# Attention on one core: sums issued singly between other VectorE work, Q fetched a tile earlier

## The chip, the cores and the metric

The kernel runs on one core of a Trainium2 chip. The metric is the device time of one execution in microseconds. TensorE does the matrix products, ScalarE (ACT) the exponentials and copies out of PSUM, VectorE (DVE) the additions, GpSimd (POOL) issues the loads, and SyncE (SP) issues the transposing DMAs and the stores. The engines run side by side, each through its own instructions in order, and wait for one another by semaphores.

## The reference

For each of 8 batches there are q, k and v of 2048 x 512 (float32):

```
scores = q @ k.T / sqrt(512)
out = softmax(scores, axis=-1) @ v
```

The kernel works in float16 with float32 sums. It leaves out the maximum in the softmax and divides by the row's sum at the end; that sum comes from a column of ones beside v.

## The kernel before, in words

**The products.** Each large product is cut into 2 x 2 blocks and done with seven block products instead of eight (Strassen-Winograd). That needs sums of blocks of the operands, made on VectorE: four instructions of 128 x 512 float16 for a chunk of K (`k_sums`, lines 138 to 145), for a query tile (`q_sums`, 147 to 154), for a chunk of V (`v_sums`, 170 to 178), and for the exponentials (`p_sums`, 274 to 284).

**Tiles and stages.** A query tile is 512 rows; a batch has four, so there are 32. Stage g (1 to 31) multiplies the exponentials of tile g by V (class `Pair`) and, interleaved with that, makes the scores of tile g+1 (class `Group`). "Kind" means g modulo 4 below: it decides which prefetches a stage carries. A full stage has 28 slots (0 to 27). In each slot one block product of the scores is issued (four matmuls of 256 columns, line 237), in each odd slot also one block product of Pair (eight matmuls, line 319), and last the prefetches that a table gives for (kind, slot). Before stage 1, a prologue loads the first batch and does tiles 0 and 1 with plain matmuls.

**One turn of the scores.** A group of 256 keys takes seven slots, in the order `QORDER` (line 368), and two of its products (7 and 4) are done in the next group's turn. At slot 1 of a turn product 7 of the group before is issued, and VectorE adds it into a buffer (line 260, which ends the use of a PSUM bank that product 4 at slot 4 writes on). At slot 2 ScalarE takes the exponential of that buffer (`exp_right`, line 272, recorded as L188 pt<-cz). At slot 4 come three of the four `p_sums` (lines 280 to 282), which wait for that exponential; at slot 5 the second addition (line 263) and the fourth (line 284).

**Pair.** A tile's output is done as two halves, a and b, in the order `ORDER` (line 366): a1 b1 a5 a3 a2 a6 a7 b5 a4 b3 b2 b6 b7 b4, at slots 1, 3, 5, ... 27. After products 5 and 3 VectorE takes a reciprocal (lines 342, 348) and ScalarE scales (line 327); after 2, 6 and 7 VectorE adds scaled halves into the output tile ("final", line 330). Product 3 has to wait for the scaling after 5, product 7 for the scaling after 6, and product 4 for the final after 7, since they write on the same PSUM banks. There are four output tiles in rotation; a tile is free again when its store (line 337) has landed.

**Prefetch.** Lines 372 to 429. Loads cast to float16 on the way from memory, into three staging buffers for Q and K (line 62) or straight into V's two buffers (line 65). A transposing DMA (line 111) then turns Q or K into its operand, from SP's queue, where the stores stand too. SP and POOL run ahead of the slots: what holds them is the order of their queues and their waits. VectorE does the sums where the table's slot puts them in its queue, four in a row. Q's tile for stage g+1's scores, number g+2, is loaded at slot 0 of stage g, transposed at slot 9 and summed at slot 21. Q's operands have three buffers (line 64).

Of the kernel before, what the change touches and what calls it, by code (L numbers as in the profile page):

```python
# [1 line left out]

# [9 lines left out]
def kernel(  # L12
# [21 lines left out]
    nc = tc.nc  # L34
    P = 128
    B, T, D = q.shape
# [10 lines left out]
    NQT = T // QTW  # L47
# [3 lines left out]
    H = D // 2  # L51
# [45 lines left out]
    def load(what, b, c):  # L97
        t = stage.tile([P, CH, D], F16, tag="stage")
        nc.gpsimd.dma_start(out=t[:], in_=srcs[what][b, :, c * CH:(c + 1) * CH, :])
        staged[what, b, c] = t  # L100
# [7 lines left out]
    def dma_transpose(what, b, c):  # L108
        src = staged.pop((what, b, c))
        t = operands(what)  # L110
        nc.sync.dma_start_transpose(
            out=t[0][:].rearrange("p n c r -> p (n c) r"),
            in_=src[:].rearrange("p n d -> p (n d)"),
        )
        (kT if what == "k" else qT)[b, c] = t
# [14 lines left out]
    def k_blocks(t):  # L130
        w = t[0][:].rearrange("p (j s) c r -> p j s c r", s=2)
        return w[:, :, 0, 0:2], w[:, :, 0, 2:4], w[:, :, 1, 0:2], w[:, :, 1, 2:4]

    def q_blocks(t):
        w = t[0]
        return w[:, 0:2, 0:2], w[:, 2:4, 0:2], w[:, 0:2, 2:4], w[:, 2:4, 2:4]

    def k_sums(b, c):
        t = kT[b, c]
        a11, a12, a21, a22 = k_blocks(t)  # L140
        _, s1, s2, s4 = t
        nc.vector.tensor_add(s1[:], a21, a22)
        nc.vector.tensor_sub(a21, a11, a21)
        nc.vector.tensor_sub(s2[:], s1[:], a11)
        nc.vector.tensor_sub(s4[:], a12, s2[:])

    def q_sums(b, c):
        t = qT[b, c]
        b11, b12, b21, b22 = q_blocks(t)
        _, t1, t2, t4 = t  # L150
        nc.vector.tensor_sub(t1[:], b12, b11)
        nc.vector.tensor_sub(b12, b22, b12)  # L152
        nc.vector.tensor_sub(t2[:], b22, t1[:])
        nc.vector.tensor_sub(t4[:], b21, t2[:])  # L154

    def new_v(b):
        vh = vpool.tile([P, NJ, 2, VP], F16, tag="vh")
        t1 = vpool.tile([P, NJ, TP], F16, tag="t1")
        t2 = vpool.tile([P, NJ, H], F16, tag="t2")
        t4 = vpool.tile([P, NJ, H], F16, tag="t4")  # L160
        nc.gpsimd.memset(vh[:, :, 1, D:D + 1], 1.0)
        nc.gpsimd.memset(t1[:, :, H:H + 1], 1.0)
        vs[b] = (vh, t1, t2, t4)

    def load_v(b, c):
        dst = vs[b][0][:].rearrange("p j s d -> p (j s) d")
        ns = slice(c * CH, (c + 1) * CH)
        nc.gpsimd.dma_start(out=dst[:, ns, 0:D], in_=srcs["v"][b, :, ns, :])

    def v_sums(b, c):  # L170
        vh, t1, t2, t4 = vs[b]
        js = slice(c * CH // 2, (c + 1) * CH // 2)
        b11, b12 = vh[:, js, 0, 0:H], vh[:, js, 0, H:D]
        b21, b22 = vh[:, js, 1, 0:H], vh[:, js, 1, H:D]
        nc.vector.tensor_sub(t1[:, js, 0:H], b12, b11)
        nc.vector.tensor_sub(b12, b22, b12)
        nc.vector.tensor_sub(t2[:, js], b22, t1[:, js, 0:H])
        nc.vector.tensor_sub(t4[:, js], b21, t2[:, js])

    def new_p(g):  # L180
        pt = ppool.tile([P, NJ, 2, QTW], F16, tag="pt")
# [8 lines left out]
    def plain_tile(g, kb):  # L190

        b, qt = divmod(g, NQT)
        if kb == 0:
            new_p(g)
        st = bank("qz" if kb % 3 == 2 else "qx")
        c, n = divmod(kb, CH)
        for dc in range(ND):
            nc.tensor.matmul(  # L198
                st[:], kT[b, c][0][:, n, dc, :], qT[b, qt][0][:, :, dc, :],
                start=(dc == 0), stop=(dc == ND - 1),  # L200
            )
        exp(pts[g][0][:, kb // 2, kb % 2, :], st[:])
# [71 lines left out]
    def p_sums(g, n, part=None):  # L274
        pt, s1, s2, s4 = pts[g]
        js = slice(n * G, (n + 1) * G)
        a11, a21 = pt[:, js, 0, 0:QH], pt[:, js, 0, QH:QTW]
        a12, a22 = pt[:, js, 1, 0:QH], pt[:, js, 1, QH:QTW]
        if part in (None, 0):
            nc.vector.tensor_add(s1[:, js], a21, a22)  # L280
            nc.vector.tensor_sub(s2[:, js], s1[:, js], a11)
            nc.vector.tensor_sub(a21, a11, a21)  # L282
        if part in (None, 1):
            nc.vector.tensor_sub(s4[:, js], a12, s2[:, js])  # L284
# [83 lines left out]
    QORDER = ((0, 1), (1, 7), (0, 5), (0, 6), (1, 4), (0, 3), (0, 2))  # L368
    NS = len(QORDER) * NG


    def plan():
        at = {}

        def add(qt, slot, *what):
            at.setdefault((qt, slot), []).append(what)

        for qt in range(NQT):
            add(qt, 0, "load", "q", 3)
            add(qt, 9, "trans", "q", 3)  # L380
            add(qt, 21, "qsum", "q", 3)
        add(0, 1, "newv")
        for c, (lq, ls, sq, ss) in enumerate(((0, 1, 0, 14), (0, 5, 0, 25), (1, 1, 1, 14), (1, 5, 1, 25))):
            add(lq, ls, "load", "v", c)
            add(sq, ss, "vsum", "v", c)
        add(1, 15, "load", "k", 0)
        add(1, 25, "trans", "k", 0)
        add(2, 6, "ksum", "k", 0)
        add(2, 3, "load", "k", 1)
        add(2, 13, "trans", "k", 1)  # L390
        add(2, 26, "ksum", "k", 1)
        add(2, 11, "load", "k", 2)
        add(2, 20, "trans", "k", 2)
        add(3, 4, "ksum", "k", 2)
        add(2, 18, "load", "k", 3)
        add(2, 27, "trans", "k", 3)
        add(3, 11, "ksum", "k", 3)
        return at

    PLAN = plan()  # L400

    def prefetch(g, slot):
        b, qt = divmod(g, NQT)
        todo = PLAN.get((qt, slot), [])
        if g == 1:
            todo = [x for x in PLAN.get((0, slot), ()) if x[0] == "newv" or x[1] == "v"] + todo
        for what in todo:
            if what[0] != "newv" and what[1] == "q":
                n = g + 2
                if n >= B * NQT or n < NQT:  # L410
                    continue
                bb, c = divmod(n, NQT)
            else:
                bb = b + 1
                if bb >= B:
                    continue
                c = what[2] if len(what) > 2 else 0
            if what[0] == "newv":
                new_v(bb)
            elif what[0] == "load":  # L420
                load_v(bb, c) if what[1] == "v" else load(what[1], bb, c)
            elif what[0] == "trans":
                dma_transpose(what[1], bb, c)
            elif what[0] == "ksum":
                k_sums(bb, c)
            elif what[0] == "qsum":
                q_sums(bb, c)
            elif what[0] == "vsum":
                v_sums(bb, c)


    NP = B * NQT
# [31 lines left out]
    def pv(g, n):  # L464
        pairs[ORDER[n][0] == "b"].product(int(ORDER[n][1]))

    for kb in range(NKB):
        plain_tile(1, kb)
        if kb == 3:
            dma_transpose("q", 0, 2)  # L470
        if kb == 4:
            dma_transpose("q", 0, 3)
        if 6 <= kb < 14 and kb % 2 == 0:
            v_sums(0, (kb - 6) // 2)
        if kb % (2 * G) == 0 and kb:
            p_sums(1, kb // (2 * G) - 1)
        if kb >= 14:
            pv(0, kb - 14)
    p_sums(1, NG - 1)
    for n in range(2, len(ORDER)):  # L480
        pv(0, n)
        if n < 6:
            k_sums(0, n - 2)
        if n == 6:
            q_sums(0, 2)
        if n == 7:
            q_sums(0, 3)

    prev = None
    for g in range(1, NP):  # L490
        pairs = (Pair(g, 0), Pair(g, 1))
        for slot in range(NS):
            if g + 1 < NP:
                n, at = divmod(slot, len(QORDER))
                if at == 0:
                    cur = Group(g + 1, n)
                old, what = QORDER[at]
# [6 lines left out]
            if g + 1 < NP or slot < 7:  # L504
                at = slot % len(QORDER)
# [42 lines left out]
```

## Time and profile before

| What | Value |
|---|---|
| time, three runs | 950.77 us (949.81 to 951.2) |
| the profiled execution | 956.65 us, of it 954.6 us between its first and last instruction |
| granted TensorE clock, mean | 0.975 |
| TensorE, VectorE, ScalarE, GpSimd busy | 88%, 62%, 60%, 8% of the span |
| DMA queues | 115.50 MB moved, mean 121 GB/s |

The busy share is a mean over a prologue of some 65 us, 30 stages of 25.8 to 31.4 us and a short end. Stage g was delimited by the start of the first product of its slot 0 on TensorE's timeline; stages 1 to 29 carry sums of the prefetch, stage 30 carries none. In the timeline, rows of one line that follow one another are merged, and the bracket tells how long the engine sat idle before the row and what ended that.

### The profile page before, as it was taken

The page shows a single profiled execution, that of the slowest core. Times are in us where ns is not written, and L with a number is a line of the kernel's source. Part 1 is how long each engine was busy: PE and PEld are TensorE (multiplying, and loading weights), DVE is VectorE, ACT ScalarE, POOL GpSimd, SP SyncE. Part 2 cuts the span into 40 slices and gives each one's busy share as a digit, 9 for nine tenths or more (in the row PEclk, how much of TensorE's full clock was granted, in tenths as well). Part 3 has the DMA queues.
Part 4 walks back from the last instruction along what each step waited for, and adds up shares of the span by engine and source line. Part 5 has one row for each costly group of instructions (what it writes and reads, how often), then busy time and mean ns, then how long its engine had stood idle before and what let it go on. Part 6 is the DMA issues. An engine that isn't in the chain of part 4 may idle for free.

```text
span 954.6 us, 18101 instructions
## 1 busy us (share of the span) xinstructions
PE 843.9 (88%) x7169; PEld 709.0 (74%) x7169; DVE 593.1 (62%) x1460; ACT 569.2 (60%) x1009; POOL 72.8 (8%) x116
## 2 busy tenths in 40 slices
PE   6978998899898998988989889898889899899997
PEld 4567777677776777777878778687777787777885
DVE  3767656566665676567666576656666566666553
ACT  2525656566565665666656566565656656566673
POOL 3100001000010000100001000010001000000000
PEclk9999989999998999999999999999999999999999
DMA  9992957849687484974959659395693946931111
GB/s 145 202 162 74 139 109 122 155 91 142 123 133 137 99 151 101 144 144 97 153 83 157 135 108 155 73 174 120 119 155 77 181 98 106 184 90 43 52 41 67
DMA packets 189989, 115.50 MB, mean 121 GB/s; under 512 B 124368, under 2 KB 173520, under 8 KB 189904
## 3 DMA queue, kind: packets, MB, share of 16 engines
q0 software_dynamic: 50688, 50.34, 35.6%
q1 hardware_dynamic: 139216, 64.01, 31.2%
q8 instruction: 56, 0.92, 0.4%
q14 instruction: 29, 0.24, 0.1%
HBM read 100.70 MB, written 33.55 MB: 141 GB/s over the span
## 4 chain that ended last, share of the span: by engine, by line
PE 40%; DVE 25%; ACT 15%; DMA 14%; issue 5%; POOL 0%; ACTq 0%; DVEq 0%; POOLq 0%
PE t L319 20%; PE t L237 16%; DMA raw<-t 14%; ACT pt L188 7%; ACT o L327 5%; DVE o L330 4%; PE t L198 3%; DVE cz L260 3%; DVE cz L263 3%; ACT cz L254 2%; DVE s L280 2%; DVE pt L282 1%; DVE s L284 1%; DVE raw L152 1%; DVE qs L154 1%
## 5 line engine op out<-in xcount | busy, mean ns | idle before, releaser
L319 PEld LDWEIGHTS <-pt 128*128 128x128 f16 x2048 | 204.8, 100 | 69.8 <-issue 41.8
L237 PEld LDWEIGHTS <-raw 128*128 128x128 f16 x1920 | 189.8, 99 | 69.2 <-issue 45.3
L319 PE MATMUL t<-vh,pt 128*128 128x256 f16 x1536 | 207.1, 280 | 26.3 <-ACT o L327 26.3
L327 ACT ACTIVATE o<-t,r 128x256 f32<-128x256 f32 x256 | 121.5, 475 | 180.9 <-DVE r L342 107.9
L188 ACT ACTIVATE pt<-t 128x512 f16<-128x512 f32 x272 | 163.7, 602 | 83.9 <-PE t L237 57.4
L237 PE MATMUL t<-raw 128*128 128x256 f16 x1440 | 204.1, 276 | 7.7 <-ACT pt L188 7.7
L319 PEld LDWEIGHTS <-s 128*128 128x128 f16 x1536 | 150.5, 98 | 53.5 <-issue 33.4
L330 DVE SCALAR_TENSOR_TENSOR o<-t,r,o 128x256 f32<-128x256 f32 x192 | 92.5, 482 | 114.0 <-ACT o L327 81.2
L237 PEld LDWEIGHTS <-ks 128*128 128x128 f16 x1440 | 143.8, 100 | 23.6 <-issue 1.8
L188 ACT ACTIVATE pt<-cz 128x1024 f16<-128x1024 f32 x120 | 127.4, 1061 | 47.4 <-DVE cz L260 47.4
L237 PE MATMUL t<-qs,ks 128*128 128x256 f16 x960 | 137.2, 277 | 1.0 <-DVE cz L263 1.0
L280 DVE TENSOR_TENSOR s<-pt 128x512 f16<-128x512 f16 x128 | 54.1, 422 | 129.7 <-ACT pt L188 129.7
L319 PE MATMUL t<-t,s 128*128 128x257 f16 (+1 forms) x1024 | 133.1, 273 | 0.8 <-DVE o L330 0.8
L237 PE MATMUL t<-qs,raw 128*128 128x256 f16 x480 | 72.3, 273 | 29.1 <-DVE cz L260 29.1
L260 DVE TENSOR_TENSOR cz<-t,cz 128x512 f32<-128x512 f32 x120 | 82.4, 687 | 24.3 <-PE t L237 24.1
L254 ACT COPY cz<-t 128x512 f32<-128x512 f32 x120 | 70.2, 585 | 43.3 <-PE t L237 39.2
L319 PE MATMUL t<-vh,s 128*128 128x257 f16 x512 | 68.4, 277 | 27.8 <-ACT o L327 27.8
L263 DVE TENSOR_TENSOR cz<-t,cz 128x512 f32<-128x512 f32 x120 | 81.9, 682 | 5.6 <-PE t L237 5.6
L250 ACT COPY t<-t 128x512 f32<-128x512 f32 x120 | 68.4, 570 | 23.9 <-PE t L237 21.5
L237 PE MATMUL t<-raw,ks 128*128 128x256 f16 x480 | 75.4, 281 | 0.5 <-ACT cz L254 0.5
L319 PE MATMUL t<-t,pt 128*128 128x256 f16 x512 | 68.2, 277 | 5.0 <-DVE o L330 2.1
L257 ACT COPY cz<-t 128x512 f32<-128x512 f32 x120 | 69.6, 580 | 1.9 <-PE t L237 1.8
(34 smaller groups left out, 482.7 us busy)
## 6 DMA issues: line engine op xcount, KB each, us to landing
out_dram<-o SPq DMA_DIRECT2D x128, 256.0 KB, 2.5
t<-in_q_dram POOLq DMA_DIRECT2D x32, 512.0 KB, 8.2
t<-in_k_dram POOLq DMA_DIRECT2D x32, 512.0 KB, 7.5
vh<-in_v_dram POOLq DMA_DIRECT2D x32, 512.0 KB, 14.9
raw<-t SPq DMA_TRANSPOSE x58, 7.0
ident<-attn_identity SPq DMA_DIRECT2D x1, 32.0 KB, 1.6
```

What stands on the lines that cost most here:

```text
L188: nc.scalar.activation(out=out_, in_=in_, func=EXP, scale=inv_sqrt_d)
L198: nc.tensor.matmul(st[:], kT[b, c][0][:, n, dc, :], qT[b, qt][0][:, :, dc, :], start=(dc == 0), stop=(dc == ND - 1),)
L237: nc.tensor.matmul(dst[:, j * QH:(j + 1) * QH], lhs[:, j, c, :], rhs[:, :, c, :], start=(n in (1, 5) and j == 0 and c == 0), stop=(c == 1) ...
L250: nc.scalar.copy(out=self.y[:], in_=self.x[:])
L254: nc.scalar.copy(out=self.cz[:, :, 1, :], in_=self.two(self.z))
L257: nc.scalar.copy(out=self.cz[:, :, 0, :], in_=self.two(self.x))
L260: nc.vector.tensor_add(self.cz[:, :, 1, :], self.two(self.x), self.cz[:, :, 1, :])
L263: nc.vector.tensor_add(self.cz[:, :, 0, :], self.two(self.z), self.cz[:, :, 0, :])
L280: nc.vector.tensor_add(s1[:, js], a21, a22)
L319: nc.tensor.matmul(dst[:, 0:width], lhs(j), rhs(j), start=(first and j == 0), stop=(j == NJ - 1), skip_group_check=True,)
L327: nc.scalar.activation(out=out_, in_=src, func=COPY, scale=r[:])
L330: nc.vector.scalar_tensor_tensor(out=out_, in0=src, scalar=r[:], in1=out_, op0=MULT, op1=ADD)
```

## The change

There are three edits.

1. `k_sums`, `q_sums` and `v_sums` no longer issue their four instructions, but return them as a list. The prologue runs each list at once. In the stages the list is appended to a queue, `background`, and one instruction is taken from it at the end of slots 0, 2, 3 and 6 of each turn of seven.
2. The table has Q's load at slot 0 and its transpose at slot 10 for tile g+3, and its sums, appended at slot 12 (15 in stages of kind 3), for tile g+2, which was transposed one stage earlier.
3. The other entries of the table move by a few slots: the loads of V, the sums of V (14 and 25 become 16 and 24), the loads, transposes and sums of K. The preparation of V's next buffer (`new_v`, with two memsets on POOL) comes at slot 0, ahead of Q's load, instead of at slot 1, behind it.

The number of instructions and their sizes stay as they are.

```
     def k_sums(b, c):
...
-        nc.vector.tensor_add(s1[:], a21, a22)
-        nc.vector.tensor_sub(a21, a11, a21)
-        nc.vector.tensor_sub(s2[:], s1[:], a11)
-        nc.vector.tensor_sub(s4[:], a12, s2[:])
+        return [
+            lambda: add(s1[:], a21, a22),
+            lambda: sub(a21, a11, a21),
+            lambda: sub(s2[:], s1[:], a11),
+            lambda: sub(s4[:], a12, s2[:]),
+        ]
...
+    PLAN = {}
+    for qt_, slot_, *what_ in (
+        (0, 0, "newv"),
+        (0, 2, "load", "v", 0), (0, 16, "sum", "v", 0),
+        (0, 8, "load", "v", 1), (0, 24, "sum", "v", 1),
+        (1, 2, "load", "v", 2), (1, 16, "sum", "v", 2),
+        (1, 8, "load", "v", 3), (1, 24, "sum", "v", 3),
+        (1, 16, "load", "k", 0), (1, 26, "trans", "k", 0), (2, 8, "sum", "k", 0),
+        (2, 2, "load", "k", 1), (2, 14, "trans", "k", 1), (2, 25, "sum", "k", 1),
+        (2, 8, "load", "k", 2), (2, 20, "trans", "k", 2), (3, 4, "sum", "k", 2),
+        (2, 14, "load", "k", 3), (2, 27, "trans", "k", 3), (3, 11, "sum", "k", 3),
+    ):
+        PLAN.setdefault((qt_, slot_), []).append(what_)
+    for qt_ in range(NQT):
+        PLAN.setdefault((qt_, 0), []).append(("load", "q", 3))
+        PLAN.setdefault((qt_, 10), []).append(("trans", "q", 3))
+        PLAN.setdefault((qt_, 15 if qt_ == 3 else 12), []).append(("sum", "q", 2))
+    background = deque()
...
+                background.extend({"k": k_sums, "q": q_sums, "v": v_sums}[what[1]](bb, c))
+        if background and slot % len(QORDER) in (0, 2, 3, 6):
+            background.popleft()()
```

## Rows read from the trace of the kernel before

**Rows 1.** Page, part 1: busy time, share of the span, instructions of each engine.

```profile
PE 843.9 (88%) x7169; PEld 709.0 (74%) x7169; DVE 593.1 (62%) x1460; ACT 569.2 (60%) x1009; POOL 72.8 (8%) x116
```

**Rows 2.** Waits of TensorE: us in total, times, longest us.

```profile
PE t L319 <- ACT o L327: 54.1, 66, 2.1
PE t L237 <- DVE cz L260: 29.1, 29, 2.6
```

**Rows 3.** Windows, sums over stages: six of kind 0, 1, 2; seven of kind 3.

```profile
sum 184.57, PE 161.19 PEld 136.00 DVE 108.63 ACT 108.02 POOL 22.71; mean PE 26.86 PEld 22.67 DVE 18.11 ACT 18.00 POOL 3.78
...
sum 167.57, PE 152.75 PEld 131.45 DVE 106.58 ACT 108.01 POOL 4.44; mean PE 25.46 PEld 21.91 DVE 17.76 ACT 18.00 POOL 0.74
...
sum 163.25, PE 150.74 PEld 131.32 DVE 112.52 ACT 108.51 POOL 13.76; mean PE 25.12 PEld 21.89 DVE 18.75 ACT 18.09 POOL 2.29
...
sum 216.29, PE 187.68 PEld 158.19 DVE 139.82 ACT 126.50 POOL 14.26; mean PE 26.81 PEld 22.60 DVE 19.97 ACT 18.07 POOL 2.04
```

**Rows 4.** Windows: stage 2; stages 28 and 29 summed; stage 30 (start:end, length, busy, PEclk).

```profile
91.90:122.00 30.10, 26.79 (x226) 22.75 (x224) 20.99 (x52) 18.08 (x32) 2.96 (x4) 0.94 0.90 154
...
sum 54.41, PE 50.24 PEld 43.81 DVE 31.54 ACT 36.17 POOL 0.00; mean PE 25.12 PEld 21.90 DVE 15.77 ACT 18.09 POOL 0.00
...
908.09:933.90 25.81, 24.96 (x226) 21.91 (x224) 14.26 (x35) 17.98 (x32) 0.00 (x0) 1.00 0.11 43
```

**Rows 5.** Timeline, TensorE, ends of stages 29 and 30 (start, length, work, idle before).

```profile
903.73 0.60 PE L237 MATMUL t<-qs,raw 128*128 128x256 f16 x4 [0.63 <-DVE cz L260]
905.18 1.03 PE L319 MATMUL t<-vh,pt 128*128 128x256 f16 x8 [0.85 <-ACT o L327]
...
930.99 1.03 PE L319 MATMUL t<-vh,pt 128*128 128x256 f16 x8 [0.25 <-ACT o L327]
...
933.03 1.03 PE L319 MATMUL t<-t,pt 128*128 128x256 f16 x8
```

**Rows 6.** Timeline, VectorE, stage 29: three of Q's sums and the addition behind them.

```profile
901.86 0.42 DVE L152 TENSOR_TENSOR raw<-raw 128x512 f16<-128x512 f16 x1
902.20 0.42 DVE L153 TENSOR_TENSOR qs<-raw,qs 128x512 f16<-128x512 f16 x1
902.65 0.42 DVE L154 TENSOR_TENSOR qs<-raw,qs 128x512 f16<-128x512 f16 x1
902.99 0.68 DVE L260 TENSOR_TENSOR cz<-t,cz 128x512 f32<-128x512 f32 x1
```

**Rows 7.** Timeline, VectorE, stage 30, where no prefetch sums run.

```profile
922.03 0.69 DVE L260 TENSOR_TENSOR cz<-t,cz 128x512 f32<-128x512 f32 x1 [0.30 <-PE t L237]
...
925.05 0.42 DVE L280 TENSOR_TENSOR s<-pt 128x512 f16<-128x512 f16 x1 [1.97 <-ACT pt L188]
...
928.22 0.48 DVE L330 SCALAR_TENSOR_TENSOR o<-t,r,o 128x256 f32<-128x256 f32 x1 [0.93 <-ACT o L327]
928.62 0.68 DVE L260 TENSOR_TENSOR cz<-t,cz 128x512 f32<-128x512 f32 x1
930.97 0.48 DVE L330 SCALAR_TENSOR_TENSOR o<-t,r,o 128x256 f32<-128x256 f32 x1 [1.68 <-ACT o L327]
...
932.50 0.48 DVE L330 SCALAR_TENSOR_TENSOR o<-t,r,o 128x256 f32<-128x256 f32 x1
```

**Rows 8.** Timeline, ScalarE, stage 30: the exponential behind the last addition.

```profile
929.51 1.06 ACT L188 ACTIVATE pt<-cz 128x1024 f16<-128x1024 f32 x1
```

**Rows 9.** Timeline, TensorE, stage 7 (kind 3), product a3 at slot 7.

```profile
247.34 1.67 PE L319 MATMUL t<-vh,s 128*128 128x257 f16 x8 [2.05 <-ACT o L327]
```

**Rows 10.** Windows: the stretch behind that wait (the 0.50 is the granted clock).

```profile
247.59:251.00 3.41, 3.41 (x19) 2.40 (x17) 0.86 (x2) 1.48 (x4) 0.00 (x0) 0.50 1.34 167
```

**Rows 11.** Groups by line: the first of Q's sums.

```profile
L151 DVE TENSOR_TENSOR qs<-raw 128x512 f16<-128x512 f16 x30 | 12.5, 416 | 9.2 <-DMA raw<-t 9.2
```

**Rows 12.** Chain of waits, stage 8 (kind 0): Q's transposing DMA.

```profile
271.27 21.41 DMA raw<-t
```

**Rows 13.** DMA issues from 288 to 290 us: a store, KB, us to landing.

```profile
out_dram<-o SPq DMA_DIRECT2D x1, 256.0 KB, 6.5
```

More of the change, by code (lines that the diff above doesn't have):

```diff
@@ L1 @@
+from collections import deque
 from contextlib import ExitStack
@@ L136, in q_blocks @@
         return w[:, 0:2, 0:2], w[:, 2:4, 0:2], w[:, 0:2, 2:4], w[:, 2:4, 2:4]
+    add, sub = nc.vector.tensor_add, nc.vector.tensor_sub
     def k_sums(b, c):
@@ L150, in q_sums @@
         _, t1, t2, t4 = t
[L151 to L154, printed above, removed]
+        return [
+            lambda: sub(t1[:], b12, b11),
+            lambda: sub(b12, b22, b12),
+            lambda: sub(t2[:], b22, t1[:]),
+            lambda: sub(t4[:], b21, t2[:]),
+        ]
     def new_v(b):
@@ L174, in v_sums @@
         b21, b22 = vh[:, js, 1, 0:H], vh[:, js, 1, H:D]
[L175 to L178, printed above, removed]
+        return [
+            lambda: sub(t1[:, js, 0:H], b12, b11),
+            lambda: sub(b12, b22, b12),
+            lambda: sub(t2[:, js], b22, t1[:, js, 0:H]),
+            lambda: sub(t4[:, js], b21, t2[:, js]),
+        ]
     def new_p(g):
@@ L369 @@
     NS = len(QORDER) * NG
[L372 to L400, printed above, removed]
+    PLAN = {}
+    for qt_, slot_, *what_ in (
+        (0, 0, "newv"),
[8 rows of a table added]
+    ):
[5 more added lines that the diff above has]
+    background = deque()
     def prefetch(g, slot):
@@ L407, in prefetch @@
         for what in todo:
+            bb, c = b + 1, what[-1]
             if what[0] != "newv" and what[1] == "q":
-                n = g + 2
-                if n >= B * NQT or n < NQT:
+                if not NQT <= g + what[2] < B * NQT:
                     continue
[L412 to L417, printed above, removed]
+                bb, c = divmod(g + what[2], NQT)
+            elif bb >= B:
+                continue
             if what[0] == "newv":
@@ L423, in prefetch @@
                 dma_transpose(what[1], bb, c)
[L424 to L429, printed above, removed]
+            else:
+                background.extend({"k": k_sums, "q": q_sums, "v": v_sums}[what[1]](bb, c))
+        if background and slot % len(QORDER) in (0, 2, 3, 6):
+            background.popleft()()
     NP = B * NQT
@@ L473 @@
         if 6 <= kb < 14 and kb % 2 == 0:
-            v_sums(0, (kb - 6) // 2)
+            for f in v_sums(0, (kb - 6) // 2):
+                f()
         if kb % (2 * G) == 0 and kb:
@@ L482 @@
         if n < 6:
-            k_sums(0, n - 2)
+            for f in k_sums(0, n - 2):
+                f()
         if n == 6:
-            q_sums(0, 2)
+            for f in q_sums(0, 2):
+                f()
         if n == 7:
-            q_sums(0, 3)
+            for f in q_sums(0, 3):
+                f()
     prev = None
```

## The prediction, made before the change was run

> **What bounds the kernel now.** I read the page's busy shares first: TensorE is busy 88% of the span, VectorE and ScalarE about 60% [rows 1]. So the time is TensorE's work plus what TensorE waits, and I went on to the waits of TensorE. Two lines hold nearly all of them: Pair's products wait for ScalarE's scaling, 54.1 us, and the scores' products wait for VectorE's addition of line 260, 29.1 us [rows 2]. Neither engine is full, so these are waits on the order of work and not on its amount. Then I cut the trace into stages with the windows view. Their lengths are far apart although TensorE has the same work in each: kind 0 has 184.57/6 = 30.8 us, kind 1 27.9, kind 2 27.2, kind 3 216.29/7 = 30.9 [rows 3], and stage 30, which has no sums of the prefetch, 25.81 us [rows 4]. That is the floor to compare with: same products, same exponentials, none of what the change moves. Above the floor lie 184.57 − 6 × 25.81 = 29.7 us in kind 0, likewise 12.7 in kind 1, 8.4 in kind 2, 35.6 in kind 3, and 4.3 in stage 2 and 2.8 in stages 28 and 29 [rows 3, 4]: 93.5 us in all. This is the most that the change can give.
>
> **Where a block of four sums costs.** VectorE works in order, so four sums delay whatever stands behind them by about 1.6 us.
> - Q's sums at slot 21. In stage 29 they run just ahead of the addition of line 260 [rows 6]. That addition begins 22.10 us after the stage's start (902.99 − 880.89); in stage 30 it begins at 20.53 (928.62 − 908.09) [rows 7]. It is 1.57 late, product 4 waits 0.63 for it, the exponential behind it holds up ScalarE's scaling, and product b7 waits 0.85 for that, against 0.25 in stage 30 [rows 5]. Each of stages 28 and 29 is 1.40 longer than stage 30 [rows 4]. The exponential had 0.21 of slack in stage 30 (929.51 against 928.62 + 0.68) [rows 7, 8]; 1.57 − 0.21 = 1.36, so the lateness beyond the slack goes into the stage one to one.
> - A block at slot 14 (kinds 0 and 1) or 11 (kind 3): kind 1 minus kind 2 is (167.57 − 163.25)/6 = 0.72 [rows 3]. Kind 2 has blocks at slots 6 and 26 besides Q's and is as long as stage 29, which has only Q's, so those two are free, and so is the one at slot 25 of kind 1.
> - K's sums at slot 4 (kind 3) stand ahead of a reciprocal, ScalarE scales later, and a3 waits 2.05 us [rows 9]. After it the granted clock is at 0.50, that is 1.2 instead of 2.4 GHz, for 3.41 us [rows 10], which costs up to 1.7. Kind 3's 5.1 above the floor are 1.4 (Q) + 0.7 (slot 11) + 3.0 for this place with its clock.
> - Kind 0's 4.95 are 1.4 + 0.7 + 2.85 for a wait on data: Q's first sum waits for its transpose, 9.2 us in all [rows 11], which is on the chain with 21.41 us [rows 12], and the clock falls behind that too.
>
> **The change part by part.** It adds and removes no instruction, so VectorE's 593.1 us stay.
>
> (a) Q a tile earlier. The sums take data transposed a stage before. The six waits go; nothing is late in their place, since the transpose has some 25 us more. On SP the transpose now also waits for product 4 at slot 4 of its stage (the third buffer is free only then), with the stores behind it in the queue; on POOL the load of Q in kind 0 stands behind the two memsets that wait for V's buffer. Behind the stores stands ScalarE, which scales into the output tile that a store sets free. This cover is thinner than before and is a rival below; I take it at nothing, with the bounds 0 and rival 4.
>
> (c) The other moves. The loads of K and V are held by free buffers and not by slots, so a few slots in the table change little; V's later sums have at least a stage before their use. K's loads wait for staging buffers that Q's transposes now give back some 4 us later, and the third chunk's sums begin at slot 6 of kind 3, 14 slots (some 13 us) behind its transpose in the queues. Taken as 0; if its data were late, the nearest row is the wait of Q's sums, 9.2/6 = 1.5 us a stage [rows 11].
>
> (b) The sums one at a time. I go through the places by the order of VectorE's queue, with stage 30 as the pattern. Sums in a row begin 0.34 apart, or 0.45 where one needs the one before [rows 6].
> - Slots 27, 0, 2, 3 and 6, 7, 9, 10: before and after line 260's addition VectorE has idle time, and the nearest rows are the free blocks at 6 and 26. K's block at slot 4 is among those moved here, now behind the reciprocal. Taken as 0; bound 0.36 a stage (half of 0.72).
> - Slots 13 and 14: both come ahead of line 260, which waited 0.30 for TensorE [rows 7]. It becomes 0.74 − 0.30 = 0.44 late, against 1.58 − 0.30 = 1.28 for a block of four, which costs 0.72 and so has 0.56 swallowed. Taken as 0; bound 0.36.
> - Slots 16 and 17: VectorE waits 1.97 there for an exponential [rows 7]. 0.
> - Slots 20 and 21: the first fits into the wait of 0.93 ahead of b2's final, the second comes between that and line 260's addition [rows 7]. It is 0.34 late, less the slack of 0.21: b7 waits 0.13 longer. Bound: half of Q's 1.40.
> - Slots 23 and 24 (not in kind 2, whose queue is empty by then): both stand behind b6's final and ahead of the three `p_sums` and b7's final. In stage 30 VectorE is busy without a break from b6's final at 930.97 to b7's, which ends at 932.98, and b4 begins right then, at 933.03 [rows 5, 7]. So b7's final is 0.13 + 0.74 late and b4 with it: 0.87, taken as 0.88. A block here has no row; the bounds are 0 (a block at 25 is free) and 1.6.
>
> So a stage is 25.81 + 0.88 = 26.69, in kinds 0, 1 and 3 and in stage 2 (whose queue is still full from stage 1), and 25.81 + 0.13 = 25.94 in kind 2; stages 28 and 29 have Q's sums at 13 to 17 alone and come to the floor. Gains: kind 0 184.6 − 160.1 = 24.4; kind 1 167.6 − 160.1 = 7.4; kind 2 163.3 − 155.6 = 7.6; kind 3 216.3 − 186.8 = 29.5; stage 2 3.4; stages 28 and 29 2.8: 75.1 us. Stage 1, the prologue and the end are left as they are.
>
> VectorE's spacing is also where a page of the Trainium skill says otherwise. "VectorE: DVE Perf Modes", section "The DRAIN you can't avoid", has the next operation start only when the one before has emptied the pipe. By it two sums cost 0.84 and not 0.74 at slots 23 and 24, 2 us more over 20 stages. The rows show starts 0.34 apart for instructions of 0.42 [rows 6], so the trace does not agree here.
>
> **The sum.** The profiled execution took 956.65 us, of it 2 outside the span; less 75.1 that is 881.6. The median of the runs is 950.77, 0.6% below the profiled one; less the same 75 it is 876 us, which I forecast.
>
> **Rivals.**
> 1. Everything fits: the two sums at the stage's end are hidden as well. Then all 93.5 go: 857 to 860. For it: VectorE is at 62%. Against it: the unbroken run of VectorE before b4.
> 2. The clock. In a stage of the changed kernel TensorE waits about 0.4 ahead of b7 and 1.0 ahead of b4. If the clock falls behind these as behind a3 in stage 7 [rows 10], 20 stages lose 1.4 to 1.7: 876 + 31 = 907. Against it: stage 29 waits 0.63 and 0.85 within 1.5 us [rows 5] and stages of kind 1 like it have no 0.50; for it, a single wait of 2.05 is enough. The Trainium skill, "TensorE: Matmul & The Clock Gate", section "A second HAM failure mode: psum-queue depth-cycling", has frequent short idle times between groups of matmuls make the clock swing; it speaks for this rival, and the trace bears it out only from longer waits on.
> 3. Late stores in kind 0. Q's transpose there was issued with V's loads and landed 22.5 us after the stage's start [rows 12]. It starts 3 to 8 us later now and has one more load beside it: 25.5 to 30.5. The stores stand behind it in the queue; a store of that stretch takes 6.5 [rows 13], and I let it land 3 behind the transpose. The output tile is written again at about 26.7 + 6 = 32.7. So 0 to 1 us is missing in the worse half; with 2 missing and a fall of the clock (1.7) it is 6 × 3.7 = 22: 898.
> 4. Slower than before, by the same place: the transpose holds SP so long that ScalarE waits for an output tile in every stage of kind 0 or 1. It decides from 75/6 = 12.5 us a batch on, that is with stores landing after 32.7 + 11 = 44 us (1.7 being the clock). With 14 us missing it is 876 + 6 × 15.7 = 970. Against it: the transpose would have to take over 31 us instead of 21.
> 5. The sums don't spread: single or not, VectorE reaches them late and they stand in front of line 260 as a block. Then slot 21's 1.40 stays in 20 stages, 876 + 20 × 0.6 = 888, and only the waits on data and slot 4 are gained. The idle times of VectorE around each place [rows 7] speak against it.
>
> **How the numbers follow.** Forecast (the sums cost 0.9 at the stage's end) 0.54; rival 1 0.13; rival 2 0.12; rival 3 0.12; rival 5 0.05; rival 4 0.04. The forecast's own range is 868 to 888 (0.5 to 1.4 a stage). The range for 8 in 10 takes in rivals 3 and 5 and half of rivals 1 and 2: 860 to 907. About 0.2% can be told from no change: faster 0.95, same 0.01, slower 0.04.
>
> **What would show it.** In the changed trace: no wait of Q's sums on a DMA; stages of kinds 0, 1 and 3 of equal length near 26.7 and kind 2 shorter by 0.7; no idle time of TensorE ahead of product 4 for line 260; a wait of about 1 us ahead of b4 for the final of line 330, which the trace of before does not have in its waits; fewer stretches at 0.50. Stages with b4's wait absent make rival 1 right; a 0.50 after each stage's end, rival 2; ScalarE waiting for a store at slots 5 to 8 of kind 1, rivals 3 and 4. The prediction is wrong if kind 0 stays the longest.

## The result, and the profile after

The changed kernel took **881.4 us** (median of 4 executions, 880.79 to 882.67) against 950.99 us for the kernel before in the same comparison (949.81 to 951.53): a ratio of 0.9272, 95% interval 0.9256 to 0.9288. The forecast was 876 us in a range of 860 to 907. The profiled execution took 881.62 us, of it 879.5 between its first and last instruction.

Part 1 of the page, changed kernel, beside [rows 1]: TensorE has the same 7169 matmuls, is busy 32 us less and has a greater share of a shorter span. By estimate some 24 of the 32 are the 14 stretches at half clock that are gone (14 × 3.41/2, the length of [rows 10]). The rest isn't clock: in kind 2, at a granted clock of 1.00 in both kernels, TensorE's busy time also fell, from 25.12 to 24.96 a stage.

```profile
PE 811.9 (92%) x7169; PEld 697.8 (79%) x7169; DVE 585.2 (67%) x1460; ACT 568.5 (65%) x1009; POOL 72.9 (8%) x116
```

TensorE's waits in the changed kernel (us in total, times, longest), beside [rows 2]. Line numbers have moved: 319 is now 328, 327 is 336, 330 is 339, 260 is 269. The wait of the scores' products for the addition, 29.1 us before, is gone altogether; the wait for ScalarE has fallen from 54.1 to 31.5; the wait of Pair's products for a final has grown from 2.9 us in four places (last row, kernel before) to 22.4 in 25.

```profile
PE t L328 <- ACT o L336: 31.5, 66, 1.9
PE t L328 <- DVE o L339: 22.4, 25, 0.9
```

```profile
PE t L319 <- DVE o L330: 2.9, 4, 0.9
```

The stages by kind, changed kernel, windows view, sums over the same stages as in [rows 3]: six of kind 0, six of kind 1, six of kind 2, seven of kind 3. Per stage that is 26.75, 26.76, 25.96 and 26.75 us.

```profile
sum 160.52, PE 149.77 PEld 131.29 DVE 102.83 ACT 108.38 POOL 23.61; mean PE 24.96 PEld 21.88 DVE 17.14 ACT 18.06 POOL 3.94
...
sum 160.54, PE 149.79 PEld 131.27 DVE 111.19 ACT 108.38 POOL 4.45; mean PE 24.96 PEld 21.88 DVE 18.53 ACT 18.06 POOL 0.74
...
sum 155.73, PE 149.77 PEld 131.27 DVE 110.05 ACT 107.90 POOL 13.34; mean PE 24.96 PEld 21.88 DVE 18.34 ACT 17.98 POOL 2.22
...
sum 187.28, PE 174.74 PEld 153.19 DVE 137.64 ACT 125.89 POOL 13.76; mean PE 24.96 PEld 21.88 DVE 19.66 ACT 17.98 POOL 1.97
```

Stage 2, and stages 28 and 29 summed, beside [rows 4] (start:end, length, busy times, granted clock): 27.10 instead of 30.10, and twice the floor of 25.81.

```profile
90.27:117.37 27.10, 24.95 (x226) 21.90 (x224) 19.66 (x52) 17.98 (x32) 2.22 (x3) 1.00 0.93 143
...
sum 51.62, PE 49.92 PEld 43.76 DVE 31.19 ACT 35.94 POOL 0.00; mean PE 24.96 PEld 21.88 DVE 15.59 ACT 17.97 POOL 0.00
```

The end of stage 8 (kind 0) on TensorE's timeline, beside [rows 5]: product 4 of the scores (first row) has no wait, b7 waits 0.40 and b4 0.93.

```profile
272.39 0.60 PE L246 MATMUL t<-qs,raw 128*128 128x256 f16 x4
273.39 1.03 PE L328 MATMUL t<-vh,pt 128*128 128x256 f16 x8 [0.40 <-ACT o L336]
...
276.23 1.03 PE L328 MATMUL t<-t,pt 128*128 128x256 f16 x8 [0.93 <-DVE o L339]
```

The same end on VectorE's timeline, beside [rows 7]. The first row is b6's final, the last b7's. Two of V's sums (lines 185, 186) stand between them, and VectorE has no gap from the first to the last; b4 starts 0.06 us after the last row ends.

```profile
273.37 0.48 DVE L339 SCALAR_TENSOR_TENSOR o<-t,r,o 128x256 f32<-128x256 f32 x1 [1.49 <-ACT o L336]
273.77 0.42 DVE L185 TENSOR_TENSOR t<-vh,t 128x512 f16<-128x512 f16 x1
274.22 0.42 DVE L186 TENSOR_TENSOR t<-vh,t 128x512 f16<-128x512 f16 x1
274.56 0.42 DVE L289 TENSOR_TENSOR s<-pt 128x512 f16<-128x512 f16 x1
...
275.69 0.48 DVE L339 SCALAR_TENSOR_TENSOR o<-t,r,o 128x256 f32<-128x256 f32 x1
```

Product a3 of stage 7, beside [rows 9]: 0.47 us instead of 2.05.

```profile
230.34 1.04 PE L328 MATMUL t<-vh,s 128*128 128x257 f16 x8 [0.47 <-ACT o L336]
```

Q's first sum, beside [rows 11]: its wait on the transpose is 0.7 us once, where it was 9.2.

```profile
L157 DVE TENSOR_TENSOR qs<-raw 128x512 f16<-128x512 f16 x30 | 12.3, 412 | 0.7 <-DMA raw<-t 0.7
```

DMA issues of stage 8, beside [rows 12, 13]: Q's transpose, issued at 254.45, and the first store behind it, issued at 262.68 (us to landing in the last column). The transpose is about as slow as before, but nothing waits for it.

```profile
raw<-t SPq DMA_TRANSPOSE x1, 19.1
...
out_dram<-o SPq DMA_DIRECT2D x1, 256.0 KB, 12.2
```

The next store, issued at 268.3, and ScalarE's first scaling in stage 9 on its timeline, which writes on the tile that this store frees:

```profile
out_dram<-o SPq DMA_DIRECT2D x1, 256.0 KB, 8.2
```

```profile
283.33 0.47 ACT L336 ACTIVATE o<-t,r 128x256 f32<-128x256 f32 x1 [1.33 <-DVE r L351]
```

The mean granted clock of the profiled execution is 1.000 (0.975 before); from 13 us on, no stretch of it is at 0.50.

### The profile page after: what moved, and what is told of

Read it like the earlier page. It is cut to its first block, busy times and chain, and to the rows that moved or that the text cites. A ratio compares the mean times of both kernels' runs of the same rounds, so it can differ in the third digit from the quotient of the medians.

```text
span 879.5 us, 18122 instructions
## 1 busy us (share of the span) xinstructions
PE 811.9 (92%) x7169; PEld 697.8 (79%) x7169; DVE 585.2 (67%) x1460; ACT 568.5 (65%) x1009; POOL 72.9 (8%) x116
## 4 chain that ended last, share of the span: by engine, by line
PE 61%; DVE 15%; ACT 14%; DMA 6%; issue 4%; POOL 0%; POOLq 0%; DVEq 0%; ACTq 0%
PE t L328 33%; PE t L246 28%; ACT pt L197 7%; ACT o L336 5%; DVE o L339 4%; DMA raw<-t 2%; DVE cz L272 2%; ACT cz L263 2%; DVE cz L269 2%; DMA t<-in_q_dram 2%; DVE s L289 2%; DMA t<-in_k_dram 2%; DVE pt L291 1%; DVE s L293 1%; DVE s L290 1%
## 5 line engine op out<-in xcount | busy, mean ns | idle before, releaser
L328 PEld LDWEIGHTS <-pt 128*128 128x128 f16 x2048 | 199.8, 98 | 71.8 <-issue 48.6
L328 PE MATMUL t<-vh,pt 128*128 128x256 f16 x1536 | 198.9, 273 | 14.0 <-ACT o L336 14.0
L246 PEld LDWEIGHTS <-raw 128*128 128x128 f16 x1920 | 187.7, 98 | 22.1
L246 PE MATMUL t<-raw 128*128 128x256 f16 x1440 | 196.7, 273 | 0.0
L246 PEld LDWEIGHTS <-ks 128*128 128x128 f16 x1440 | 140.8, 98 | 16.5
L246 PE MATMUL t<-qs,ks 128*128 128x256 f16 x960 | 134.3, 273 | 0.0
L289 DVE TENSOR_TENSOR s<-pt 128x512 f16<-128x512 f16 x128 | 54.1, 423 | 95.7 <-ACT pt L197 95.7
L328 PE MATMUL t<-t,pt 128*128 128x256 f16 x512 | 66.3, 272 | 22.8 <-DVE o L339 21.6
L246 PE MATMUL t<-raw,ks 128*128 128x256 f16 x480 | 72.1, 273 | 0.0
```

The costliest lines, as they stand in the source:

```text
L246: nc.tensor.matmul(dst[:, j * QH:(j + 1) * QH], lhs[:, j, c, :], rhs[:, :, c, :], start=(n in (1, 5) and j == 0 and c == 0), stop=(c == 1) ...
L328: nc.tensor.matmul(dst[:, 0:width], lhs(j), rhs(j), start=(first and j == 0), stop=(j == NJ - 1), skip_group_check=True,)
```

## The experiments

Eight kernels ran in two jobs, each compared with the kernel before on its own chip (median 952.5 and 952.2 us there).

**The kernel before, again** (no edit).

> The kernel before, unchanged, to see how its executions differ among themselves. Theory A (the time of one execution goes with the number of stretches in which the granted clock is at 0.50): executions with a higher mean clock are shorter; the profiled execution with 14 such stretches (mean clock 0.975) took 956.65 us and the others about 951, so the others should have a mean clock of about 0.98 and some 3 stretches fewer, at 1.7 us each. Theory B (the profiled execution was longer for another reason, such as DMA): the mean clock is 0.975 in all of them and does not go with the time. Median 951 by both.

Median 951.3 us, ratio 0.999 (0.997 to 1.0009). This execution took 952.62 us; the row is its span and mean clock.

```profile
core 0: 950.5 us, clock 0.978
```

Over the 23 executions of this kernel in the job, time and mean clock go together: the shortest, 947.86 us, has 0.984, the longest, 956.37, has 0.973; at 0.98 they lie between 950.8 and 953.0. Theory A holds. The trace that the prediction rests on was one of the long ones: it has 14 stretches of 3.4 us at 0.50, the trace of this run 12. Two stretches fewer are 3.4 us at 1.7 each, of the 4.0 us by which this execution is shorter (956.65 − 952.62).

**Single issue alone**: the changed kernel with the table of the kernel before.

```
-        (0, 0, "newv"),
-        (0, 2, "load", "v", 0), (0, 16, "sum", "v", 0),
...
+        (0, 0, "load", "q", 2), (0, 9, "trans", "q", 2), (0, 21, "sum", "q", 2),
+        (0, 1, "newv"),
+        (0, 1, "load", "v", 0), (0, 14, "sum", "v", 0),
...
```

> Sums issued singly, but the table of the kernel before (Q two tiles ahead, its sums from slot 21 on). My theory: in kind 0 Q's first sum stands at slot 21 and waits some 2 us for its transpose, which holds line 260's addition, and the clock falls behind that: kind 0 about 30 us. Two sums in front of b7's final in all kinds, kind 2 too: 26.7 us in kinds 1, 2 and 3. In all 881 + 6 x 3.5 + 6 x 0.75 = 907 us. Rival (Q's lead is not needed once the sums are single): kind 0 like the others, 886 us.

894.7 us, ratio 0.9396 (0.9359 to 0.9432): between the 907 of the theory and the 886 of the rival. VectorE's timeline in stage 8 shows the wait on data, now in front of a single sum, and with the addition of line 269 behind it:

```profile
273.55 0.42 DVE L157 TENSOR_TENSOR qs<-raw 128x512 f16<-128x512 f16 x1 [1.75 <-DMA raw<-t]
273.89 0.68 DVE L269 TENSOR_TENSOR cz<-t,cz 128x512 f32<-128x512 f32 x1
```

Windows, kinds 0 and 2: 28.5 and 26.6 us a stage. Kind 2 is as expected; in kind 0 the wait is there and costs its 1.86 us over 26.62, but the clock fell in one stage only, and it was expected in all six. So beside single sums Q's lead is worth 170.88 − 6 × 26.62 = 11.2 us in kind 0, in this execution.

```profile
sum 170.88, PE 152.24 PEld 132.18 DVE 102.54 ACT 108.51 POOL 19.44; mean PE 25.37 PEld 22.03 DVE 17.09 ACT 18.08 POOL 3.24
...
sum 159.74, PE 149.77 PEld 131.38 DVE 107.71 ACT 108.51 POOL 13.35; mean PE 24.96 PEld 21.90 DVE 17.95 ACT 18.09 POOL 2.23
```

**Q's lead alone**: the kernel before with

```
-            add(qt, 9, "trans", "q", 3)
+            add(qt, 10, "trans", "q", 3)
...
-                n = g + 2
+                n = g + (2 if what[0] == "qsum" else 3)
```

> The kernel before with Q loaded and transposed three tiles ahead; sums in blocks of four at the slots of before. My theory: only the wait on Q's transpose and the clock behind it go, in six stages of kind 0, which become 25.81 + 1.40 + 0.72 = 27.9 us instead of 30.8; the rest stays: 951 - 17 = 934 us. Rival (the lead is what brings most of the gain): below 915 us. Rival (the wait on data only moves to another place): 951 us.

930.7 us, ratio 0.9775 (0.9731 to 0.982). Windows, kinds 0 and 3: kind 0 is at 27.87 us as expected. Kind 3, where the edit removes no wait, went from 216.29 to 209.61: a3 waits 2.05 as before, but the clock fell behind it in one stage of seven, where it was five. In both traces stage 11 has a stretch at 0.50 near its end instead, behind product 4's wait of 0.99 (0.98 here) and b7's of 0.85. Why fewer stages fall here is open.

```profile
sum 167.24, PE 152.44 PEld 131.26 DVE 102.43 ACT 108.02 POOL 22.51; mean PE 25.41 PEld 21.88 DVE 17.07 ACT 18.00 POOL 3.75
...
sum 209.61, PE 181.01 PEld 154.87 DVE 140.41 ACT 126.13 POOL 13.39; mean PE 25.86 PEld 22.12 DVE 20.06 ACT 18.02 POOL 1.91
```

**One block moved by two slots**: the kernel before with

```
-        add(3, 4, "ksum", "k", 2)
+        add(3, 6, "ksum", "k", 2)
```

> The kernel before with one block, the sums of K's third chunk, at slot 6 instead of slot 4 of kind 3, that is behind the reciprocal of line 342 instead of ahead of it. My theory: the block is free there, a3's wait falls from 2.05 to 0.47 us and the clock stays up; kind 3 becomes 25.81 + 1.40 + 0.72 = 27.9 us instead of 30.9: 951 - 21 = 930 us. Rival (the place does not matter, VectorE's lateness is handed on): 948 us or more.

930.5 us, ratio 0.9775 (0.9732 to 0.9818). Kind 3 is at 195.43/7 = 27.92 us. Where a block of four stands in VectorE's queue, ahead of a reciprocal or behind it, is worth 216.29 − 195.43 = 20.9 us by itself, clock included.

```profile
sum 195.43, PE 178.03 PEld 153.11 DVE 140.38 ACT 126.02 POOL 13.85; mean PE 25.43 PEld 21.87 DVE 20.05 ACT 18.00 POOL 1.98
```

**The changed kernel, again** (no edit).

> The changed kernel, unchanged, as the measure for the three others of this job. 881 us, granted clock 1.00 in every stage, and executions within 2 us of each other, since no stretch at 0.50 is left to vary (the theory that such stretches make the kernel before vary by 8 us). If they vary as much as the kernel before's, that theory is wrong.

881.4 us, 880.97 to 882.26; the four mean clocks are 0.999 to 1.000. The spread is 1.3 us, against 4.3 us for the seven executions of the kernel before in the same job.

**The stage's end freed**: the changed kernel with

```
-        if background and slot % len(QORDER) in (0, 2, 3, 6):
+        if background and slot in (0, 2, 3, 6, 7, 9, 10, 13, 14, 16, 17, 20, 21, 25, 26, 27):
```

> The changed kernel with the sums of slots 23 and 24 at slots 25 and 26 instead, that is behind b7's final and not ahead of it. My theory: the 0.93 us wait of b4 comes from these two sums alone; 0.80 us goes in each of 20 stages, all kinds at 25.95: 881.4 - 16 = 865 us. Rival (VectorE is simply late at the stage's end, and the lateness is handed on to line 269's addition at slot 1 of the next stage): 873 us or more.

866.0 us, ratio to the kernel before 0.9098 (0.9079 to 0.9118). TensorE's waits: the one for a final falls from 22.4 us in 25 places to 2.9 in four, which lie outside stages 1 to 30 (three in the prologue, one at the kernel's end). Kinds 0, 1 and 2 are at 25.95 us a stage, and kind 3 too but for stage 27 (26.37). The two sums of slots 23 and 24 were the whole of b4's wait, and nothing is handed on.

```profile
PE t L328 <- ACT o L336: 31.0, 66, 1.4
...
PE t L328 <- DVE o L339: 2.9, 4, 0.9
```

**The stage's end loaded twice**: the changed kernel with

```
-        if background and slot % len(QORDER) in (0, 2, 3, 6):
-            background.popleft()()
+        for _ in range({20: 0, 21: 0, 23: 2, 24: 2}.get(slot, slot % len(QORDER) in (0, 2, 3, 6))):
+            if background:
+                background.popleft()()
```

> The changed kernel with four sums between b6's final and b7's final (two at slot 23, two at slot 24) and none at slots 20 and 21. My theory: b7 waits 0.25 again, b4 waits 0.93 + 0.75 = 1.7 us; kinds 0, 1 and 3 at 25.81 + 1.49 = 27.3, kind 2 (two sums there) at 26.55: 881.4 + 20 x 0.55 + 6 x 0.6 = 896 us. Rival (clock): a wait of 1.7 us takes the granted clock down to 0.50 behind it in most of these 20 stages, 1.4 to 1.7 us each: 920 us or more.

899.1 us, ratio 0.9441 (0.9422 to 0.9459). TensorE, stage 8: b4 waits 1.72. Then the windows of kinds 0 and 3: 27.40 a stage in kind 0, and in kind 3 too but for stage 3 (28.93), where K's sums come late out of the queue, which is still long from stage 1: a product of the scores waits 1.98 for them (third fence), and the clock falls behind that. In the 19 stages with the wait of 1.72 it doesn't fall.

```profile
282.58 1.03 PE L328 MATMUL t<-t,pt 128*128 128x256 f16 x8 [1.72 <-DVE o L339]
```

```profile
sum 164.37, PE 149.76 PEld 131.28 DVE 103.01 ACT 107.79 POOL 19.90; mean PE 24.96 PEld 21.88 DVE 17.17 ACT 17.97 POOL 3.32
...
sum 193.33, PE 176.27 PEld 154.03 DVE 138.96 ACT 125.28 POOL 17.48; mean PE 25.18 PEld 22.00 DVE 19.85 ACT 17.90 POOL 2.50
```

```profile
142.10 0.61 PE L246 MATMUL t<-qs,ks 128*128 128x256 f16 x4 [1.98 <-DVE ks L148]
```

**Two more steps**: the kernel with the stage's end freed, also without sums at slots 20 and 21 from stage 4 on, and the reciprocal of line 351 ahead of the fourth sum of exponentials.

```
-        if background and slot % len(QORDER) in (0, 2, 3, 6):
+        if background and (slot in (0, 2, 3, 6, 7, 9, 10, 13, 14, 16, 17, 25, 26, 27) or g < 4 and slot in (20, 21)):
...
-                    if at == 5:
-                        p_sums(prev.g, prev.n, 1)
...
                 pv(g, slot // 2)
+            if slot % len(QORDER) == 5 and prev is not None and (g + 1 < NP or slot < 7):
+                p_sums(prev.g, prev.n, 1)
```

> The changed kernel with no sums at slots 20, 21, 23 and 24 from stage 4 on (slots 25 and 26 take some), and the reciprocal of line 351 ahead of the fourth of the sums of exponentials at slot 5. My theory: b7 waits 0.25, b4 is not late, and a3's wait at slot 7 falls from 0.47 to about 0.13 since the reciprocal comes 0.33 earlier; all kinds at 25.5 us: 881.4 - 20 x 1.25 - 6 x 0.45 - 2 = 851 us. Rival (a3 waits for ScalarE for another reason than the reciprocal): slot 7 stays at 0.47 and the time is 860 us.

853.1 us, ratio 0.896 (0.8937 to 0.8983), the fastest here. In kinds 0 to 2 every stage is at 25.46 to 25.49 us, below the floor of 25.81, which holds only with the reciprocal in its old place. TensorE's wait for ScalarE's scaling is down to 13.5 us, and a3 in stage 7 carries no wait on the timeline (second fence). Stage 27 took 27.92 in this execution; one of K's sums waited 2.4 us for its transpose there, and no run looks into that.

```profile
PE t L328 <- ACT o L336: 13.5, 37, 1.1
```

```profile
250.09 1.04 PE L246 MATMUL t<-raw 128*128 128x256 f16 x8
251.25 1.04 PE L328 MATMUL t<-vh,s 128*128 128x257 f16 x8
```

## Why the prediction was right, and the step that was off

**The floor and the blocks.** Stage 30 as the measure was right: stages 28 and 29 come to it exactly, and moving one block by two slots took off the 3.0 us a stage that the prediction had put on its place, clock included.

**Q a tile earlier (a).** The wait on the transpose went, and nothing was late in its place. Alone it was expected at 17 us and gave 21.8 (952.5 − 930.7). Trace against trace, kind 0 gave 17.3, and most of the rest is clock: 6.7 in kind 3 and 1.4 in stage 2 (30.10 to 28.72), where this execution has fewer stretches at 0.50.

**The sums one at a time (b).** Slots 27 and 0 to 17 were taken at nothing, and in stages 2 to 30 the trace has no wait of TensorE other than a3's, b7's and b4's. A wait for a final is not quite as new as the prediction says: the trace of before has it in four places, 2.9 us, in the prologue and at the kernel's end. Slots 20 and 21 were put at 0.13; b7's wait rose from 0.25 to 0.40. Slots 23 and 24 were put at 0.74; the three starts 273.77, 274.22 and 274.56 show 0.79, since in this pair the second needs the first. Together 0.94 a stage was measured (26.75 − 25.81), where 0.88 stood. The Trainium skill's rule ("VectorE: DVE Perf Modes", "The DRAIN you can't avoid"), as the prediction put it, would have made it 0.97; the measurement lies between, and starts 0.34 apart behind instructions of 0.42 differ from that rule. The prediction left out that the same section lets an operation that is not held start earlier; it gives no figure for it.

**The other moves (c)** were taken at nothing, and no sum of K or V waits for data in the changed trace. No run made them by themselves. Nor did any run put the blocks of four whole at free places, so what issuing singly gives beyond a better place is not shown.

**The sum.** The gains by kind, with forecast ahead of measured: kind 0 24.4, 24.1; kind 1 7.4, 7.0; kind 2 7.6, 7.5; kind 3 29.5, 29.0; stage 2 3.4, 3.0; stages 28 and 29 2.8, 2.8. Stage 1, left out, gave 1.3 (26.6 to 25.3) and the prologue 0.3. Span against span it is 75.1 us, the figure forecast, and 956.65 − 75.1 = 881.6 is the profiled execution's time. An agreement that close is luck: the stages counted gave 1.7 us less than forecast, and stage 1 and the prologue, which were left out, gave 1.6.

**The step that was off** is the last one, "the median of the runs is 950.77, 0.6% below the profiled one; less the same 75 it is 876 us". The 5.4 us by which the forecast was low all come from it. The profiled execution of the kernel before had more stretches at half clock than executions near the median (mean clock 0.975 against 0.98). The change takes these stretches away whatever their number, so the gain against the median run is smaller by just the difference, and the 881.6 of the sum should have been carried over as it stood. The executions of the unchanged kernel (time going with mean clock, 14 stretches against 12) and the narrow spread of the changed one show this.

**The rivals.** Everything fits (1): no, b4's wait was there; freeing the stage's end shows what it would have been worth, 15 us. The clock (2): it didn't fall behind 0.40 and 0.93, nor with 1.72 in the same place, in 19 stages. But the prediction's case against this rival overlooked two stages: in the kernel before, the clock fell near the end of stages 2 and 11, where the waits were 0.99 and 0.85, little longer than the 0.63 and 0.85 that it cited. Stage 11 on TensorE's timeline, kernel before (b7 takes 1.66 instead of 1.03):

```profile
382.42 0.60 PE L237 MATMUL t<-qs,raw 128*128 128x256 f16 x4 [0.99 <-DVE cz L260]
383.88 1.66 PE L319 MATMUL t<-vh,pt 128*128 128x256 f16 x8 [0.85 <-ACT o L327]
```

The Trainium skill's rule on short idle times ("TensorE: Matmul & The Clock Gate", "A second HAM failure mode: psum-queue depth-cycling") fits these two stages. It is not borne out by the stages of the changed kernel: TensorE has two or three short waits in each, at a granted clock of 1.00.

Late stores (3, 4): the transpose landed 23.2 us after the start of stage 8, the store behind it at 274.9 and the next one at 276.5. The tile that this next one frees is the first to be written again, at 283.33, so 6.8 us were to spare, and ScalarE waited there for the reciprocal and not for a store. The sums as a block (5): no product waited for line 269.

## What to carry to other kernels

In a kernel whose engines are all below full, ask of every background instruction which instruction stands behind it in its engine's queue and who waits for that one. The same four sums cost 0, 0.7, 1.4 or 3 us here by their place alone (of the 3, half is clock: with Q's lead alone, the stages of kind 3 at a granted clock of 1.00 took 29.46, and with the block moved 27.92), and a stage without them gives the slack of each place. When a change removes stalls that bring the clock down, add its gains to the execution that was profiled, and don't carry them over to a median with fewer such stretches.

## What the runs showed of the hardware that was not expected

A wait of the same length in the same place is not always followed by half clock. a3's wait of 2.05 us in kind 3 was followed by 0.50 in five stages of seven in the profiled execution of the kernel before, and in one of seven with Q's lead alone; the single wait of 1.98 was followed by it, and 1.72 in 19 stages never. Nor does the longest single wait decide: two waits of 0.99 and 0.85 close together were followed by 0.50 in stages 2 and 11 of the kernel before, and with single issue alone 1.10 and 0.85 were in one stage of kind 0, while 1.24 and 0.85 in two others were not. So executions of a kernel with such waits differ by up to 8.5 us (947.86 to 956.37, 23 executions), and those of the changed kernel, in whose two traces no stretch is at 0.50, by 1.9 (880.79 to 882.67, eight executions).
